# Where the sums of w_down's quadrants are formed: in the steps of the down-projection or in those of the up-projection

## The chip, the cores and the metric

The kernel runs on one core of one Trainium2 chip. The core has a matrix engine (TensorE, PE in the profile; its weight loads are PEld), a vector engine (VectorE, DVE), a scalar engine (ScalarE, ACT), a general engine (GpSimd, POOL) and a sync engine (SyncE, SP) that here only issues DMA transfers; POOL issues some as well. The metric is the device time of one execution in microseconds, the median of a few runs.

## The reference, cut to what matters

One layer of a bidirectional encoder on 2048 tokens of width 1024: a normalised input projection, windowed attention beside a state-space branch, an output projection with residual, and then a gated feed-forward block with a convolution of width 3 over the tokens. The change lies in the feed-forward block:

```
    h = rms_norm(x, norm_ffn_g)                                # [2048, 1024]
    up = depthwise_conv(h @ w_up, conv_w, conv_b)              # [2048, 5632]
    gate, val = up[..., :2816], up[..., 2816:]
    x = x + (silu(gate) * val) @ w_down                        # w_down [2816, 1024]
    return rms_norm(x, norm_final_g)
```

All arrays are float32.

## The kernel before, in words

The first 800 us or so compute everything up to the feed-forward block. The block is one loop, `steps`, of 68 steps and a last half step. Steps 0 to 43 are the up-projection: 22 feature blocks of 128 gate and 128 value features for the first 1024 tokens, then the same 22 for the second 1024. Steps 44 to 67 are the down-projection, in three chunks of w_down's rows (`DN` = 3, 4, 4 and `DF` = 0, 6, 14: a chunk c has 2 x DN[c] blocks of 128 rows, starting at block DF[c]), each chunk in eight steps of two token blocks of 128. A chunk's result is added to that of the chunk before, which lies in DRAM (x1_d, then sum_d; `rest` loads it), and the last chunk ends in the final norm (`last_rows`).

Each step is a product of 2 x 2 quadrants done with seven products of quadrants in place of eight, in the manner of Strassen and Winograd. One side (the stationary operand, `stationary`) is formed anew in each step from what the step loads: the weights of w_up (`uraw`, two loads of 512 KB) or the activations (`araw`). The other side (the moving operand, seven tiles `self.bop`, names in `BOP`) stays for a whole run of steps: quadrants of the normalised tokens in the up-projection, quadrants of w_down and their sums in the down-projection. Four of the seven are sums: t1, t2, t3, t4. Each operand is split into a high and a low part (`...h` by ACT at L1026, `...l` by DVE at L1027), and every product of quadrants is made of three passes, high by high, high by low and low by high (L1091).

The seven products of a step are interleaved by hand with the two (numbers 4 and 3) left over from the step before; `cur` is the step, `old` the one before. Their results meet in two sets of three PSUM banks (px, py, pz) and are added up by DVE (L1111 to L1134); L1131 is the addition that frees py for product 4. In the up-projection `up_conv` then does the convolution and the gate for the step before, and POOL stores the activations to DRAM (L1202, one store for each of the 44 steps). In chunks 0 and 1 of the down stage POOL stores the partial sums (L1141).

At the last step of a run of steps, `put` re-loads each of the seven moving operands for the next run as soon as its last product is done: from DRAM into a raw buffer (`braw`, L995), split by ACT (L997) and DVE (L998). The raw buffers are three, of 512 KB, in the pool `fr`.

`down_sums(c)` forms the sums t1 to t4 of w_down's quadrants for chunk c, in DN[c] parts. A part takes all three buffers of `fr` (tag `braw`, names `bsum`): A and B are loaded with one row block of 128 from the upper and the lower half of the chunk (L1066, SP, 512 KB each); C is empty. Four DVE subtractions and additions of 128 x 512 follow (L1067 to L1070), and POOL stores the four sums to DRAM (L1072, 256 KB each), from where `put` loads them. `sums` chains the parts of the three chunks, eleven in all, and after each step whose number is in `SUMS` one `next(sums)` writes one part into the program: behind steps 26, 30 and 34 the three parts of chunk 0, behind 45 to 48 the four of chunk 1, behind 53 to 56 the four of chunk 2.

The order of the instructions on an engine, and that of the DMA issues on SP and POOL, is fixed before the run by the tile framework, which may move an instruction ahead of others that are written before it where its inputs and buffers allow; on the chip each engine goes through its list in order and waits on semaphores. A tile gets its buffer when the last user of the buffer's tile before is done.

Of the kernel before, what the change touches and what calls it, by code (L numbers as in the profile page):

```python
# [39 lines left out]
TAB = [1] * 16  # L40
DN = [3, 4, 4]
DF = [0, 6, 14]
SUMS = [26, 30, 34, 45, 46, 47, 48, 53, 54, 55, 56]
HALF = 512
BLK = 1024
BOP = ["11", "t2", "21", "t1", "t3", "t4", "22"]
# [9 lines left out]
class Net:  # L56
# [1001 lines left out]
    def down_sums(self, c):  # L1058

        nc = self.nc  # L1060
        V = nc.vector
        n, f0 = DN[c], DF[c]
        for k in range(n):
            A, B, C = (self.fr.tile([128, 2, HALF], F32, tag="braw", name=self.nm("bsum")) for _ in range(3))
            for t, f in ((A, f0 + k), (B, f0 + n + k)):
                nc.sync.dma_start(t.rearrange("p n c -> p (n c)"), self.a["w_down"][128 * f:128 * (f + 1), :])  # L1066
            V.tensor_tensor(C[:, 0], A[:, 1], A[:, 0], op=ALU.subtract)  # L1067
            V.tensor_tensor(C[:, 1], B[:, 1], A[:, 1], op=ALU.subtract)
            V.tensor_tensor(A[:, 0], C[:, 1], A[:, 0], op=ALU.add)
            V.tensor_tensor(B[:, 0], B[:, 0], A[:, 0], op=ALU.subtract)  # L1070
            for m, t in (("t1", C[:, 0]), ("t3", C[:, 1]), ("t2", A[:, 0]), ("t4", B[:, 0])):
                nc.gpsimd.dma_start(self.wsum_d[c][m][:, k], t)  # L1072
            yield

    def steps(self, p, ps):
# [21 lines left out]
        for n, at in enumerate(todo + [None]):  # L1097
# [37 lines left out]
            if old:  # L1135
# [6 lines left out]
                else:  # L1142
                    self.last_rows(f_, old["gc"], p, 2)
            if n in SUMS:
                next(sums)
# [188 lines left out]
```

## Time and profile before

| what | value |
|---|---|
| median of 3 runs | 2186.12 us (2183.91 to 2192.61) |
| the profiled execution | 2188.02 us, span 2186.2 us |
| PE busy | 2074.0 us, 95% of the span |
| PE weight load busy | 1672.5 us, 77% |
| DVE busy | 1738.7 us, 80% |
| ACT busy | 1048.1 us, 48% |
| POOL busy | 140.4 us, 6% |
| mean granted TensorE clock | 0.982 of full speed |
| data moved | 337.97 MB, 155 GB/s |

The profiled execution is one run with the hardware profiler; its span is from the first to the last instruction, and its own time has a little around that. Busy shares are means over stages with different limits, so the views below go by stretches. A busy PE need not be a PE at full speed: the granted clock stands beside it. In rows of a timeline the bracket at the end is the idle time of that engine in front of the instruction, with what ended it.

### The profile page before, as it was taken

How to read it: one execution, taken by the hardware profiler on the slowest of the kernel's cores; microseconds unless marked ns; L12 is line 12 of the kernel's file. 1: busy time of each engine (PE TensorE's matmuls, PEld its weight loads, DVE VectorE, ACT ScalarE, POOL GpSimd, SP SyncE). 2: the span in 40 equal slices, each digit the busy share in tenths (PEclk: the TensorE clock that was granted, in tenths of full speed). 3: DMA queues.
4: the chain of work that ended last, by engine and by line, in shares of the span. 5: the costliest groups of instructions: out<-in, count | busy, mean ns of one | idle time of the engine just before them, and what ended most of it. 6: DMA issues, size and time to landing. Idle time of an engine off the chain costs nothing.

```text
span 2186.2 us, 27988 instructions
## 1 busy us (share of the span) xinstructions
PE 2074.0 (95%) x10000; PEld 1672.5 (77%) x10000; DVE 1738.7 (80%) x3065; ACT 1048.1 (48%) x1836; POOL 140.4 (6%) x230
## 2 busy tenths in 40 slices
PE   7998889799999997999999999999999999899997
PEld 5777777577777776888888878888888777777786
DVE  8978888675566557888888899888888978767875
ACT  5424444776666654544444464444445424224332
POOL 1300000000000000000000001000000010100111
PEclk9999999999999998999999999999999999999999
DMA  8965665523243238422222254322222798777542
GB/s 282 338 189 154 194 179 169 162 94 92 78 130 116 82 102 256 157 82 82 78 87 87 87 183 164 130 87 85 80 87 70 248 315 292 265 230 231 187 158 93
DMA packets 208939, 337.97 MB, mean 155 GB/s; under 512 B 13856, under 2 KB 135200, under 8 KB 208800
## 3 DMA queue, kind: packets, MB, share of 16 engines
q1 hardware_dynamic: 189072, 270.58, 39.4%
q0 software_dynamic: 16288, 62.92, 7.6%
q10 hardware_dynamic: 3440, 2.69, 0.4%
q8 instruction: 78, 1.28, 0.3%
q14 instruction: 61, 0.50, 0.1%
HBM read 231.81 MB, written 104.33 MB: 154 GB/s over the span
## 4 chain that ended last, share of the span: by engine, by line
issue 40%; PE 14%; POOL 2%; DMA 2%; DVE 1%; ACT 0%; POOLq 0%; ACTq 0%; SPq 0%; DVEq 0%
PE py L1091 6%; PE px L1091 4%; PE pz L1091 4%; POOL act L1202 1%; DMA braw<-ws2t 1%; POOL sum L1141 0%; POOL ws1t L1072 0%; DMA bsum<-in_w_down_dram 0%; DMA braw<-in_w_down_dram 0%; POOL ws0t L1072 0%; DMA ws2t<-bsum 0%; POOL ws2t L1072 0%; DVE bt L998 0%; DVE cu L1131 0%; ACT bt L997 0%
## 5 line engine op out<-in xcount | busy, mean ns | idle before, releaser
L1091 PE MATMUL px<-b,g1h 128*128 128x512 f32 x1056 | 328.6, 392 | 1.4 <-ACT cu L1109 1.4
L1091 PEld LDWEIGHTS px<-b,g1h 128*128 128x128 f32 x1056 | 199.9, 190 | 43.8 <-ACT cu L1109 2.3
L1091 PE MATMUL px<-b,g1l 128*128 128x512 f32 x528 | 207.6, 393 | 5.6 <-DVE g1l L1027 5.6
L1091 PE MATMUL py<-bt,g2h 128*128 128x512 f32 x528 | 168.4, 400 | 14.9 <-DVE cu L1131 14.9
L1091 PE MATMUL py<-bt,s2h 128*128 128x512 f32 x528 | 164.5, 393 | 4.0 <-ACT s2h L1026 4.0
L1091 PE MATMUL pz<-bt,s1h 128*128 128x512 f32 x528 | 163.2, 389 | 3.4 <-ACT s1h L1026 3.4
L1091 PE MATMUL pz<-b,s4h 128*128 128x512 f32 x528 | 162.9, 389 | 0.0
L1091 PE MATMUL py<-bt,s1h 128*128 128x512 f32 x528 | 162.7, 389 | 0.0
L1091 PEld LDWEIGHTS py<-bt,g2h 128*128 128x128 f32 x528 | 101.3, 193 | 39.5 <-DVE cu L1131 12.5
L1026 ACT ACTIVATE s1h<-st 128x1024 fp32r<-128x1024 f32 (+1 forms) x68 | 70.4, 1035 | 121.5 <-PE py L1091 108.1
L1091 PEld LDWEIGHTS px<-b,g1l 128*128 128x128 f32 x528 | 100.2, 190 | 28.5 <-DVE g1l L1027 7.5
L1091 PEld LDWEIGHTS py<-bt,s2h 128*128 128x128 f32 x528 | 98.9, 189 | 27.3 <-ACT s2h L1026 7.3
L1091 PEld LDWEIGHTS pz<-bt,s1h 128*128 128x128 f32 x528 | 99.0, 188 | 24.3 <-ACT s1h L1026 3.8
L1091 PEld LDWEIGHTS py<-bt,s1h 128*128 128x128 f32 x528 | 99.1, 188 | 20.6
L1091 PEld LDWEIGHTS pz<-b,s4h 128*128 128x128 f32 x528 | 99.1, 188 | 20.6
L78 PE MATMUL po<-wo,oh 128*128 128x512 f32 x256 | 112.2, 438 | 0.0
L1116 DVE TENSOR_TENSOR cu<-py,cu 128x512 f32<-128x512 f32 x68 | 46.9, 690 | 79.4 <-PE py L1091 79.3
L1091 PE MATMUL py<-bt,s2l 128*128 128x512 f32 x264 | 104.0, 394 | 2.4 <-DVE s2l L1027 2.2
L1091 PE MATMUL py<-bt,g2l 128*128 128x512 f32 x264 | 105.3, 399 | 0.0
L80 PE MATMUL po<-wo,ol 128*128 128x512 f32 x256 | 103.1, 403 | 0.0
L1091 PE MATMUL pz<-b,s4l 128*128 128x512 f32 x264 | 102.7, 389 | 0.0
L1091 PE MATMUL pz<-bt,s1l 128*128 128x512 f32 x264 | 102.7, 389 | 0.0
(272 smaller groups left out, 5070.4 us busy)
## 6 DMA issues: line engine op xcount, KB each, us to landing
uraw<-in_w_up_dram SPq DMA_DIRECT2D x88, 512.0 KB
araw<-act SPq DMA_DIRECT2D x32, 512.0 KB
xr<-sum SPq DMA_DIRECT2D x32, 512.0 KB
xr<-in_xT_dram SPq DMA_DIRECT2D x30, 512.0 KB
braw<-bop_d SPq DMA_DIRECT2D x28, 512.0 KB
act<-cv POOLq DMA_DIRECT2D x22, 512.5 KB, 2.9
bsum<-in_w_down_dram SPq DMA_DIRECT2D x22, 512.0 KB
act<-cv POOLq DMA_DIRECT2D x22, 511.5 KB, 3.3
```

The source lines that it names most:

```text
L78: nc.tensor.matmul(out, sh, mh, start=first and i == 0, stop=False)
L80: nc.tensor.matmul(out, sl, mh, start=False, stop=last and i == n - 1)
L1026: S.activation(h[:, :c], src, AF.Copy)
L1091: nc.tensor.matmul(bank, x[:, k], o[:, y, k], start=first and k == 0 and i == 0, stop=k == kn - 1 and i == 2, skip_group_check=True)
L1116: V.tensor_tensor(old["vc"][:, lo], old["Y"], old["vc"][:, lo], op=ALU.add)
L1202: nc.gpsimd.dma_start(self.act_d[c][f - DF[c], :, cols], va)
```

## The change

The list `SUMS` and one `yield`. Each part of `down_sums` is now written in two pieces: the two loads behind one step, the four DVE instructions and four stores behind the next. The eleven parts are written behind the pairs of steps 2 and 3, 5 and 6, 8 and 9, 11 and 12, 14 and 15, 17 and 18 (first 1024 tokens: the three parts of chunk 0 and three of chunk 1), and 24 and 25, 27 and 28, 30 and 31, 33 and 34, 36 and 37 (second 1024 tokens: the last of chunk 1 and the four of chunk 2). Nothing is computed that was not before, and nothing is left out.

```
-SUMS = [26, 30, 34, 45, 46, 47, 48, 53, 54, 55, 56]
+SUMS = [f + i for f in (2, 5, 8, 11, 14, 17, 24, 27, 30, 33, 36) for i in (0, 1)]
...
             A, B, C = (self.fr.tile([128, 2, HALF], F32, tag="braw", name=self.nm("bsum")) for _ in range(3))
             for t, f in ((A, f0 + k), (B, f0 + n + k)):
                 nc.sync.dma_start(t.rearrange("p n c -> p (n c)"), self.a["w_down"][128 * f:128 * (f + 1), :])
+            yield
             V.tensor_tensor(C[:, 0], A[:, 1], A[:, 0], op=ALU.subtract)
             V.tensor_tensor(C[:, 1], B[:, 1], A[:, 1], op=ALU.subtract)
             V.tensor_tensor(A[:, 0], C[:, 1], A[:, 0], op=ALU.add)
```

## Rows read from the trace of the kernel before

**Rows 1.** Stretches: busy us (count) of PE, PEld, DVE, ACT, POOL; clock, DMA share, GB/s.

```profile
1000.00:1280.00 280.00, 280.00 (x1237) 231.83 (x1236) 234.12 (x279) 130.33 (x181) 8.10 (x15) 1.00 0.26 91
1320.00:1380.00 60.00, 60.00 (x266) 49.47 (x265) 59.57 (x81) 30.05 (x40) 8.09 (x15) 1.00 0.50 171
1390.00:1690.00 300.00, 300.00 (x1325) 248.51 (x1324) 254.75 (x332) 145.06 (x189) 8.33 (x16) 1.00 0.24 82
1740.00:1800.00 60.00, 56.92 (x244) 45.07 (x244) 50.46 (x82) 14.09 (x23) 12.93 (x24) 1.00 0.92 320
1870.00:1930.00 60.00, 53.10 (x218) 42.78 (x217) 42.93 (x63) 13.36 (x18) 11.87 (x22) 0.94 0.79 257
1930.00:1990.00 60.00, 60.00 (x266) 49.67 (x266) 40.27 (x54) 14.50 (x19) 3.19 (x6) 1.00 0.65 204
```

**Rows 2.** Timeline of PE, 1740 to 1930 us, matmuls with idle time before them.

```profile
1778.22 0.74 PE L1091 MATMUL py<-bt,s2h 128*128 128x512 f32 x2 [0.86 <-ACT s2h L1026]
1792.83 0.50 PE L1091 MATMUL px<-b,g1l 128*128 128x512 f32 x1 [1.31 <-DVE g1l L1027]
1795.45 0.73 PE L1091 MATMUL py<-bt,s2h 128*128 128x512 f32 x2 [0.74 <-ACT s2h L1026]
1840.10 1.05 PE L1091 MATMUL py<-bt,g2h 128*128 128x512 f32 x2 [2.70 <-DVE cu L1131]
1846.96 0.73 PE L1091 MATMUL px<-b,g1h 128*128 128x512 f32 x2 [0.43 <-ACT cu L1109]
1864.60 1.19 PE L1091 MATMUL py<-bt,g2h 128*128 128x512 f32 x2 [4.11 <-DVE cu L1131]
1890.24 0.50 PE L1091 MATMUL py<-bt,s2l 128*128 128x512 f32 x1 [2.07 <-DVE s2l L1027]
1918.31 0.81 PE L1091 MATMUL py<-bt,g2h 128*128 128x512 f32 x2 [4.84 <-DVE cu L1131]
```

**Rows 3.** Timeline of DVE, first instruction of four of the parts.

```profile
1784.93 0.69 DVE L1067 TENSOR_TENSOR bsum<-bsum 128x512 f32<-128x512 f32 x1 [3.91 <-DMA bsum<-in_w_down_dram]
1888.29 0.69 DVE L1067 TENSOR_TENSOR bsum<-bsum 128x512 f32<-128x512 f32 x1 [5.11 <-DMA bsum<-in_w_down_dram]
1901.55 0.69 DVE L1067 TENSOR_TENSOR bsum<-bsum 128x512 f32<-128x512 f32 x1 [3.68 <-DMA ws2t<-bsum]
1916.96 0.69 DVE L1067 TENSOR_TENSOR bsum<-bsum 128x512 f32<-128x512 f32 x1 [6.48 <-DMA bsum<-in_w_down_dram]
```

**Rows 4.** Chain of waits, 1904 to 1934 us: start, duration, what.

```profile
1904.34 5.66 DMA ws2t<-bsum
...
1910.14 6.73 DMA bsum<-in_w_down_dram
...
1931.11 2.72 PE py L1091 x12
```

**Rows 5.** Short stretches behind gaps of PE; columns as in rows 1.

```profile
1890.00:1896.00 6.00, 5.76 (x18) 4.58 (x19) 6.00 (x10) 0.00 (x0) 1.32 (x3) 0.72 0.74 218
...
1840.00:1844.00 4.00, 3.90 (x10) 3.08 (x11) 3.19 (x5) 2.12 (x2) 0.00 (x0) 0.57 1.00 365
```

**Rows 6.** Stretches, tile bsum alone: busy us (count) of DVE, POOL; clock, DMA.

```profile
1320.00:1380.00 60.00, 8.18 (x12) 6.48 (x12) 1.00 0.50 171
1740.00:1930.00 190.00, 22.00 (x32) 17.29 (x32) 0.96 0.86 292
```

**Rows 7.** Timelines of DVE and PE in one step of the first half.

```profile
1111.50 0.68 DVE L1131 TENSOR_TENSOR cu<-py,cu 128x512 f32<-128x512 f32 x1
...
1116.31 0.62 PE L1091 MATMUL py<-bt,g2h 128*128 128x512 f32 x2
```

**Rows 8.** Timelines of POOL and DVE: activation stores, a part of chunk 0.

```profile
1369.49 0.54 POOL L1202 DMA_DIRECT2D act<-cv  x1 [10.60 <-DVE cv L1199]
1370.84 0.69 DVE L1067 TENSOR_TENSOR bsum<-bsum 128x512 f32<-128x512 f32 x1
...
1735.49 0.53 POOL L1202 DMA_DIRECT2D act<-cv  x1 [17.00 <-DVE cv L1199]
```

More of the change, by code (lines that the diff above doesn't have):

```diff
@@ L42 @@
 DF = [0, 6, 14]
-SUMS = [26, 30, 34, 45, 46, 47, 48, 53, 54, 55, 56]
+SUMS = [f + i for f in (2, 5, 8, 11, 14, 17, 24, 27, 30, 33, 36) for i in (0, 1)]
 HALF = 512
@@ L1066, in down_sums @@
                 nc.sync.dma_start(t.rearrange("p n c -> p (n c)"), self.a["w_down"][128 * f:128 * (f + 1), :])
+            yield
             V.tensor_tensor(C[:, 0], A[:, 1], A[:, 0], op=ALU.subtract)
```

## The prediction, made before the changed kernel was run

> **What bounds the kernel now.** I read the busy time by stretch first. In the up-projection TensorE (PE) is busy for every microsecond of the long stretches, 280.00 of 280.00 and 300.00 of 300.00, at the full granted clock [rows 1]. There only more work on PE's path, or a wait that reaches PE, can change the time. In the down stage two stretches differ: 56.92 of 60 us (1740 to 1800) and 53.10 of 60 us with a granted clock of 0.94 (1870 to 1930). The stretch behind them, with the same seven products a step and no sums, is full again: 60.00 of 60 [rows 1]. These two are the stretches in which the sums of chunks 1 and 2 run.
>
> Second, the timeline of PE, read only for idle time in front of a matmul. Between 1740 and 1930 us there are eight such gaps, all of them in [rows 2]. Three belong to the re-loading of the operands between chunk 0 and chunk 1 (2.70, 0.43 and 4.11 us). The other five, 0.86, 1.31, 0.74, 2.07 and 4.84 us, stand where the sums run.
>
> Third, the timeline of VectorE (DVE) at the sums [rows 3]. DVE works in order. At the first subtraction of a part (L1067) it stood still for 3.91, 5.11 and 6.48 us until the load of w_down had landed, and for 3.68 us until a store of the part before had landed. Behind that instruction stood s2l and g1l (the split stationaries) and the addition at L1131, and PE's gaps end on exactly these: 1792.83 on g1l, 1890.24 on s2l, 1918.31 on L1131 [rows 2]. So the chain is: store of part k lands, SP may issue the loads of part k+1 into the same three buffers, the load lands, DVE goes on, PE goes on. At 1916.96 the chain of waits shows it whole: 5.66 us of store, 6.73 us of load, then L1067 [rows 4].
>
> A stall is not a gap of its own length: 5.11 us cost PE 2.07 us and 6.48 us cost 4.84, while the 3.68 us at 1901.55 cost nothing. The steps of chunk 0, with three blocks in place of four, forgive less: 3.91 us cost 1.31 + 0.74.
>
> **What is removed.** Of the eleven parts, the eight of chunks 1 and 2 leave the down stage (chunk 0 was in the up-projection already). With them go the stalls, so these gaps: 0.86 + 1.31 + 0.74 + 2.07 + 4.84 = 9.82 us. Two of them were followed by a stretch at the lower clock: from 1890 to 1896 and from 1918 to 1924 the granted clock is 0.72 [rows 5], part of it at 1.2 in place of 2.4 GHz (one of the two windows stands there; the other reads the same 0.72). That is (1 - 0.72) x 6 = 1.68 us of lost matmul time each, 3.36 us together. Sum: 13.2 us. Lower bound: if the three short gaps in chunk 0, which are near to what an ordinary late split costs, stay, 10.3 us. SP also loses 16 loads there and POOL 32 store issues (17.29 us with their 22.00 us of DVE work [rows 6]). What is late next? Nothing that reaches PE: from 1930 to 1990, with the same loads of activations and partial sums at 204 GB/s and no parts, PE does not idle [rows 1].
>
> **What is added.** The same work, 22.00 us of DVE for eight parts, is 2.75 us a part [rows 6]; it goes beside PE in the up-projection, which DVE must have room for. DVE there is busy 234.12 of 280 us in the first half of the tokens and 254.75 of 300 in the second [rows 1]. A step is seven products of 2.72 us [rows 4], 19.04 us, so DVE's idle time in a step is 45.88 / 280 x 19.04 = 3.12 us in the first half and 45.25 / 300 x 19.04 = 2.87 us in the second. A part of 2.75 us fits either, the second with 0.12 us to spare, and some of that idle time is slivers that no instruction fits into. Beyond that DVE may be late: its addition L1131 starts at 1111.50 and takes 0.68 us, and the product that needs the bank it reads starts at 1116.31 [rows 7], 4.1 us later. Zero is the low end of the cost.
>
> Will they come in successive steps? The place in the text is not the place on the chip. The three parts of chunk 0 are written behind steps 26, 30 and 34. The third of them ran at 1370.84 us, right behind the store of the activations at 1369.49; nineteen more such stores follow, the last of the 44 (step 43's) at 1735.49, so that store is step 24's [rows 8]. A part written for step 34 ran ten steps early, and all three ran within 60 us [rows 6]. The order is fixed before the run, and the parts moved up to where buffers were free. So I expect six parts one after another behind the operand loads of the first half, and five behind those of the second. That is the densest case the rows know: from 1320 to 1380 DVE was busy 59.57 of 60 us with three parts, and PE 60.00 of 60 at clock 1.00 [rows 1]. This row decides for me: three successive parts on top of DVE's backlog from the operand loads cost nothing. The up-projection also has the bandwidth: 91 and 82 GB/s against 320 and 257 in the two stretches of the sums [rows 1]; a part adds two loads of 512 KB and four stores of 256 KB, 2 MB a step or some 110 GB/s.
>
> The queues. SP's loads of a part stand among the loads of w_up, which go into four buffers, two to a step, and so run a step ahead of their use; the part's loads wait for the stores of the part before. At the worst row (5.66 us for a store [rows 4]) w_up comes that much later out of a step of 19 us: nothing. On POOL the four store issues (17.29 / 32 = 0.54 us each [rows 6]) stand ahead of an activation store that nobody needs before the down stage. The extra yield puts a part's four DVE instructions a step behind its loads in the text. If the order keeps this, no part can wait for its load; if the parts move up as before, the distance is again what the order takes a load to cost, and here the bounds lie apart. In the up-projection the three parts had 0.00 us of such waits (DVE 59.57 of 60); in the down stage up to 6.48. I take zero. In the down stage DVE had so many holes (40.27 busy of 60 [rows 1]) that parts came 13.3 and 15.4 us apart in chunk 2 [rows 3], close to the 5.66 + 6.73 us of store and load. In the up-projection one hole of 3 us a step spaces them by about 19 us, which is beyond that.
>
> **The rivals.** (a) Some parts stall DVE in the up-projection as in the down stage: the first half of the tokens has no backlog behind which a load could land. Two stalls like that at 1888 cost 2 x (2.07 + 1.68) = 7.5 us: 2180.5. For it: DVE idles there in every step. Against it: loads there meet a third of the traffic.
> (b) Slower: the same stall at its worst, 6.48 us, part after part: 4.84 + 1.68 = 6.5 us each. From two of these on the gain is gone; with four of the eleven it is 26 us, and the time 2199. It needs stores and loads to take 12.4 us in the up-projection too, against which stand 82 to 91 GB/s.
> (c) More gain: the operand loads between chunk 0 and chunk 1 meet a DMA share of 1.00 at 1840 to 1844 [rows 5], with the gaps 2.70 + 0.43 + 4.11 [rows 2]. The granted clock of 0.57 there costs (1 - 0.57) x 4 = 1.7 us behind either long gap (the window at 1864 reads the same): 10.7 us in all. If less traffic and free buffers take half of that away, the time is 2168; all, 2162. Against it: the parts of chunk 1 are done by then, and those of chunk 2 come later.
> (d) The edit moves nothing that matters: the order lets the parts of chunks 1 and 2 drift to where they were. 2186. Against it: in the trace parts moved forward, never back.
> (e) POOL's store issues hold DVE, or the other way round. An issue of 0.54 us, four to a part, would make a part 2.75 + 4 x 0.54 = 4.91 us against idle times of 3.12 and 2.87: six parts make DVE 10.7 us late and five 10.2, less 4.1 us of room each: 12.7 us, so 2186. Against it: from 1320 to 1380 twelve such issues ran beside twelve such instructions, and PE lost nothing [rows 1, 6]. The Trainium skill (SBUF — State Buffer, Who interferes with whom) states that a DVE instruction with two SBUF inputs, as all four of a part are, and a GpSimd instruction that reads SBUF take an exclusive port in turn, the later one blocked for the whole of the other. By that rule such blocking would speak against putting more sums where DVE is fullest; that trace stretch does not show it for store issues.
>
> **How the numbers follow.** The profiled execution took 2188.02 us (span 2186.2), 1.9 us over the median of the three runs, 2186.12, and inside their spread of 2183.91 to 2192.61. On its own time the sum gives 2188.0 - 13.2 = 2174.8; on the median 2186.1 - 13.2 = 2172.9. I forecast 2173, with 2168 to 2178 as the range of this case (the lower bound 10.3 gives 2175.8, the rest is the spread of runs and small shifts in the order). Chances: forecast 0.57, (a) 0.19, (b) 0.06, (c) 0.12, (d) 0.04, (e) 0.02. The range of 8 in 10 is 2163 to 2187: it reaches from nearly the whole of (c) to (d). A measurement of this kernel tells 0.5%, 10.9 us, from no change; that line is at 2175.2 and cuts the forecast's own range. I give it two thirds on the fast side (0.38), (c) whole and a little of (a): 0.52 faster, 0.41 within, 0.07 slower.
>
> **What would show it.** In the changed kernel: no L1067 after 1690 us; PE without idle time in the steps that follow the operand loads of chunks 1 and 2; granted clock 1.00 there; the parts in two dense groups, behind the operand loads of either half, with DVE near full in them and PE busy throughout. I am wrong if PE idles in front of g1l, s2l or L1131's bank in the up-projection, if L1067 waits there for a load by more than 4 us, or if the gaps of the down stage stay without the parts.

## The result, and the profile after

The changed kernel takes 2176.2 us (median of 7 runs, 2173.63 to 2178.58) against 2186.12 us (median of 7, 2181.12 to 2192.61): 0.9948 of the time before, with a 95% interval of 0.9931 to 0.9965. That is 9.9 us less, with 13.2 forecast, inside the forecast's range of 2168 to 2178, 3 us above its middle, and right at the line of 0.5%. The profiled execution took 2178.58 us, 9.44 less than that of before. Behind this sum stand two terms, a larger gain than forecast and a loss that was forecast as zero.

In the new line numbers everything from the first subtraction on is one higher (L1067 is now L1068, L1091 is L1092, L1131 is L1132). Stretches of the changed kernel, columns as in [rows 1]:

```profile
900.00:1030.00 130.00, 124.71 (x535) 100.41 (x534) 114.15 (x145) 53.53 (x77) 16.27 (x30) 0.99 0.52 177
1320.00:1420.00 100.00, 100.00 (x442) 82.56 (x441) 98.33 (x135) 47.21 (x63) 13.64 (x26) 1.00 0.52 181
...
1740.00:1800.00 60.00, 58.90 (x247) 48.05 (x248) 48.46 (x76) 16.70 (x26) 4.80 (x9) 0.94 0.68 217
1870.00:1930.00 60.00, 60.00 (x263) 49.44 (x263) 42.83 (x58) 15.81 (x21) 3.20 (x6) 0.99 0.55 173
```

The two stretches of the down stage that had holes [rows 1] have none now that the sums would explain: the second is full, and what is left of the first, 1.10 us in front of a matmul at 1743.28 and the clock of 0.94, comes 3 us behind a gap of 3.25 us at 1739.91, where the re-loading in front of chunk 0 ends. The kernel before has the same gap at 1734.11, just ahead of its stretch. The new hole is in the first line: from 900 to 1030 us, where the six parts of the first half run, TensorE idles 5.29 of 130 us. The second line is the group of parts in the second half; DVE is nearly full there, and TensorE does not idle.

Which instructions wait? Timeline of DVE in the changed kernel, first subtraction of parts 3 to 6 and of two parts in the second half, with the instructions between parts 3 and 4:

```profile
932.79 0.69 DVE L1068 TENSOR_TENSOR bsum<-bsum 128x512 f32<-128x512 f32 x1 [3.00 <-DMA ws0t<-bsum]
...
946.99 0.68 DVE L1070 TENSOR_TENSOR bsum<-bsum,bsum 128x512 f32<-128x512 f32 x1
947.71 0.69 DVE L1071 TENSOR_TENSOR bsum<-bsum,bsum 128x512 f32<-128x512 f32 x1
948.32 0.68 DVE L1117 TENSOR_TENSOR cu<-py,cu 128x512 f32<-128x512 f32 x1
948.92 0.68 DVE L1027 TENSOR_TENSOR g2l<-uraw,g2h 128x512 fp32r<-128x512 f32 x1
950.32 1.28 DVE L1187 SCALAR_TENSOR_TENSOR cv<-cu,cw,cv 128x1023 f32<-128x1023 f32 x1 [0.72 <-ACT cv L1185]
954.40 0.69 DVE L1068 TENSOR_TENSOR bsum<-bsum 128x512 f32<-128x512 f32 x1 [2.80 <-DMA ws0t<-bsum]
...
976.25 0.69 DVE L1068 TENSOR_TENSOR bsum<-bsum 128x512 f32<-128x512 f32 x1 [3.03 <-DMA ws1t<-bsum]
...
997.93 0.69 DVE L1068 TENSOR_TENSOR bsum<-bsum 128x512 f32<-128x512 f32 x1 [2.87 <-DMA ws1t<-bsum]
...
1387.91 0.69 DVE L1068 TENSOR_TENSOR bsum<-bsum 128x512 f32<-128x512 f32 x1 [0.35 <-DMA ws2t<-bsum]
...
1407.03 0.69 DVE L1068 TENSOR_TENSOR bsum<-bsum 128x512 f32<-128x512 f32 x1 [0.63 <-DMA ws2t<-bsum]
```

Four parts wait 2.80 to 3.03 us, and not for a load: for a store of the part before. The timelines of POOL and of SP's queue beside them show which:

```profile
947.97 0.54 POOL L1073 DMA_DIRECT2D ws0t<-bsum  x1 [1.86 <-DVE bsum L1070]
948.70 0.54 POOL L1073 DMA_DIRECT2D ws0t<-bsum  x1 [0.18 <-issue]
...
947.70 0.33 SPq L1066 DMA_DIRECT2D bsum<-in_w_down_dram  x1
...
953.19 0.33 SPq L1066 DMA_DIRECT2D bsum<-in_w_down_dram  x1
```

The three buffers of a part come free one after the other: that of C when L1070 ends (947.67), and A of the next part is loaded into it at 947.70; that of A when the store issued at 947.97 has landed, and the next B is loaded there at 953.19; that of B last, when the store issued at 948.70 has landed. This last one becomes the next C, which nothing loads, but which the first subtraction writes. DVE reaches L1068 at 951.60 and stands until 954.40, 5.7 us behind the issue of the store.

With that, as an estimate from these rows, a step of 19.04 us grows by 2.75 us of part and 3.0 us of wait, less 3.12 us of idle time: 2.63 us. That gives 21.67 us; the parts above are 21.61, 21.85 and 21.68 us apart. From the first of these waits on DVE has no room left to be late, and TensorE waits. Timeline of PE in the changed kernel, the matmuls with idle time before them:

```profile
940.67 0.50 PE L1092 MATMUL py<-bt,s2l 128*128 128x512 f32 x1 [0.90 <-DVE s2l L1027]
957.48 0.50 PE L1092 MATMUL px<-b,g1l 128*128 128x512 f32 x1 [0.21 <-DVE g1l L1027]
960.63 0.73 PE L1092 MATMUL py<-bt,s2h 128*128 128x512 f32 x2 [0.59 <-ACT s2h L1026]
962.29 0.50 PE L1092 MATMUL py<-bt,s2l 128*128 128x512 f32 x1 [0.92 <-DVE s2l L1027]
984.13 0.50 PE L1092 MATMUL py<-bt,s2l 128*128 128x512 f32 x1 [0.91 <-DVE s2l L1027]
1001.01 0.50 PE L1092 MATMUL px<-b,g1l 128*128 128x512 f32 x1 [0.25 <-DVE g1l L1027]
1004.17 0.73 PE L1092 MATMUL py<-bt,s2h 128*128 128x512 f32 x2 [0.60 <-ACT s2h L1026]
1005.81 0.50 PE L1092 MATMUL py<-bt,s2l 128*128 128x512 f32 x1 [0.92 <-DVE s2l L1027]
```

These are 5.30 us in all. Six of the eight end on s2l and g1l, the split stationaries that stand behind the parts on DVE (4.11 us), two on s2h, which ACT splits from a sum that DVE forms (1.19 us).

To weigh loss and gain against each other I use three spans of each profiled execution. A runs from the first of the 44 activation stores on POOL to the ninth (the first group of parts), B from the ninth to the last (the rest of the up-projection), C from the last to the end of the span (the down stage). The time up to the first store is left out: between single profiles it varies from 901 to 911 us, in work that no kernel here changes, but for part 1: in the changed kernel its first instruction runs at 896.77 us, ahead of that store. The kernels of the experiments stand in the same table; each ratio is to the kernel before on the same chip.

| kernel | A | B | C | profiled execution | median | ratio, 95% |
|---|---|---|---|---|---|---|
| before | 150.20 | 677.25 | 450.71 | 2188.02 | 2186.12 | |
| after | 158.36 | 676.91 | 435.51 | 2178.58 | 2176.20 | 0.9948, 0.9931 to 0.9965 |
| e1_dense | 149.62 | 676.62 | 436.95 | 2167.15 | 2170.83 | 0.9929, 0.9916 to 0.9942 |
| e2_paced | 150.11 | 676.25 | 432.27 | 2170.30 | 2168.51 | 0.9919, 0.9904 to 0.9933 |
| e3_noyield | 157.41 | 677.79 | 438.04 | 2177.85 | 2177.42 | 0.9955, 0.9938 to 0.9973 |
| e4_inplace | 149.07 | 677.99 | 435.09 | 2172.35 | 2167.84 | 0.9920, 0.9906 to 0.9934 |
| e5_down_paced | 149.83 | 677.66 | 433.73 | 2174.42 | 2168.38 | 0.9918, 0.9904 to 0.9933 |
| e6_second | 149.95 | 677.32 | 453.84 | 2194.16 | 2191.02 | 1.0014, 1.0002 to 1.0026 |
| e7_more_work | 153.74 | 677.36 | 434.99 | 2169.60 | 2175.91 | 0.9951, 0.9933 to 0.9968 |
| e8_empty_first | 157.01 | 676.13 | 434.22 | 2174.96 | 2173.70 | 0.9942, 0.9926 to 0.9958 |
| e9_paced_inplace | 149.62 | 676.66 | 438.94 | 2167.99 | 2165.17 | 0.9903, 0.9886 to 0.9919 |

For the change that is 8.16 us lost in A, 0.34 gained in B and 15.20 gained in C. With the 2.0 us by which its first store came earlier they make the 9.4 us between the two profiled executions.

TensorE's own steps show more finely where the time went. The table has the start of the product of s4 in the same step of both profiled executions (matmul pz<-b,s4h on PE), and in one row the last activation store:

| place | before | after | the changed kernel is |
|---|---|---|---|
| ahead of the four waits | 912.30 | 909.21 | 3.09 us earlier |
| behind the last gap of the first group | 1007.50 | 1013.65 | 6.15 us later |
| last activation store | 1735.49 | 1741.29 | 5.80 us later |
| early in chunk 0 | 1754.10 | 1761.98 | 7.88 us later |
| chunk 0, behind the sums that ran there before | 1830.66 | 1833.38 | 2.72 us later |
| chunk 1, ahead of the stalls | 1876.68 | 1878.85 | 2.17 us later |
| chunk 1, behind them | 1925.50 | 1916.93 | 8.57 us earlier |
| chunk 2, behind the re-loading | 2064.66 | 2055.19 | 9.47 us earlier |

In the first half TensorE lost 9.24 us, 1.1 more than A shows: the first store, at which A begins, came only 2.02 us earlier where TensorE was 3.09 us ahead, as part 1 ran in front of it on DVE. The gaps alone do not make this up, because a gap costs more than its length: the step with the one gap of 0.90 us lasts 20.24 us (928.25 to 948.49), 1.20 more than 19.04. Behind that gap the next matmul of the pass comes 0.80 us later (940.67 to 941.47), where the others come 0.68 apart.

### The profile page after: what moved, and what is told of

Same layout as the page of the kernel before. It is cut to its first block, busy times and chain, and to the rows that moved or that the text cites. A ratio compares the mean times of both kernels' runs of the same rounds, so it can differ in the third digit from the quotient of the medians.

```text
span 2176.8 us, 27985 instructions
## 1 busy us (share of the span) xinstructions
PE 2077.6 (95%) x10000; PEld 1675.0 (77%) x10000; DVE 1741.6 (80%) x3065; ACT 1047.9 (48%) x1836; POOL 142.0 (7%) x230
## 4 chain that ended last, share of the span: by engine, by line
PE 46%; DVE 5%; issue 4%; DMA 3%; ACT 1%; POOL 1%; POOLq 0%; ACTq 0%; DVEq 0%
PE py L1092 20%; PE px L1092 13%; PE pz L1092 13%; DMA braw<-bop_d 1%; DMA braw<-in_w_down_dram 1%; DMA braw<-ws2t 1%; DVE b L998 1%; DVE bt L998 0%; ACT bt L997 0%; DVE cv L1187 0%; DVE cu L1132 0%; DMA braw<-ws1t 0%; DVE s1l L1027 0%; DMA ws1t<-bsum 0%; DVE g1l L1027 0%
## 5 line engine op out<-in xcount | busy, mean ns | idle before, releaser
L1092 PE MATMUL px<-b,g1h 128*128 128x512 f32 x1056 | 329.7, 393 | 2.5 <-ACT cu L1110 2.5
L1092 PEld LDWEIGHTS px<-b,g1h 128*128 128x128 f32 x1056 | 200.6, 190 | 45.3 <-ACT cu L1110 3.4
L1092 PE MATMUL px<-b,g1l 128*128 128x512 f32 x528 | 207.9, 394 | 3.7 <-DVE g1l L1027 3.7
L1092 PE MATMUL py<-bt,g2h 128*128 128x512 f32 x528 | 164.1, 391 | 9.1 <-DVE cu L1132 9.0
L1092 PE MATMUL py<-bt,s2h 128*128 128x512 f32 x528 | 166.6, 397 | 2.9 <-ACT s2h L1026 2.9
L1092 PE MATMUL pz<-bt,s1h 128*128 128x512 f32 x528 | 163.5, 390 | 3.2 <-ACT s1h L1026 3.2
L1092 PE MATMUL pz<-b,s4h 128*128 128x512 f32 x528 | 163.0, 389 | 1.0 <-DVE cu L1133 1.0
L1092 PE MATMUL py<-bt,s1h 128*128 128x512 f32 x528 | 162.7, 389 | 0.0
L1092 PEld LDWEIGHTS py<-bt,g2h 128*128 128x128 f32 x528 | 98.8, 188 | 32.3 <-DVE cu L1132 6.5
L1092 PEld LDWEIGHTS py<-bt,s2h 128*128 128x128 f32 x528 | 100.4, 191 | 26.4 <-ACT s2h L1026 5.5
L1092 PEld LDWEIGHTS px<-b,g1l 128*128 128x128 f32 x528 | 100.3, 190 | 26.3 <-DVE g1l L1027 5.3
L1092 PEld LDWEIGHTS pz<-bt,s1h 128*128 128x128 f32 x528 | 99.1, 188 | 24.5 <-ACT s1h L1026 4.0
L1092 PEld LDWEIGHTS pz<-b,s4h 128*128 128x128 f32 x528 | 99.0, 188 | 22.0 <-DVE cu L1133 1.5
L1092 PEld LDWEIGHTS py<-bt,s1h 128*128 128x128 f32 x528 | 99.1, 188 | 20.6
L1092 PE MATMUL py<-bt,s2l 128*128 128x512 f32 x264 | 105.3, 399 | 3.6 <-DVE s2l L1027 3.6
L1092 PE MATMUL py<-bt,g2l 128*128 128x512 f32 x264 | 103.1, 390 | 0.0
L1092 PE MATMUL pz<-b,s4l 128*128 128x512 f32 x264 | 102.7, 389 | 0.0
L1092 PE MATMUL pz<-bt,s1l 128*128 128x512 f32 x264 | 102.7, 389 | 0.0
L1092 PE MATMUL py<-bt,s1l 128*128 128x512 f32 x264 | 102.7, 389 | 0.0
```

The source lines that it names most:

```text
L1092: nc.tensor.matmul(bank, x[:, k], o[:, y, k], start=first and k == 0 and i == 0, stop=k == kn - 1 and i == 2, skip_group_check=True)
```

## The experiments

Theory: where the sums stand matters only through DVE's waits. The order, fixed beforehand, puts the first subtraction of a part where the store of the part before has not landed, and DVE, in order, holds the splits back. Rivals: the DVE work of the parts is itself too much for a dense group of steps; the store and load traffic slows the up-projection; the `yield`, in the wrong place, causes the wait; and for the gain: the down stage has no room for the sums at all, so that only moving them helps.

**One part in each step, placed behind an addition (e1_dense).** `issue_after` keeps what is written under it behind the instruction `mark` in the order. In each of the steps 3 to 8 and 25 to 29 the DVE instructions of one part are written, with the loads of the next behind them: groups as dense as those of the change, but at a fixed place in the step.

```
-SUMS = [f + i for f in (2, 5, 8, 11, 14, 17, 24, 27, 30, 33, 36) for i in (0, 1)]
+SUMS = [f + i for f in (2, 3, 4, 5, 6, 7, 24, 25, 26, 27, 28) for i in (0, 1)]
...
-                V.tensor_tensor(vc[:, hi], Z, vc[:, lo], op=ALU.add)
+                mark = V.tensor_tensor(vc[:, hi], Z, vc[:, lo], op=ALU.add).ins
...
-            if n in SUMS:
-                next(sums)
+            for _ in range(SUMS.count(n)):
+                with self.tc.issue_after(mark):
+                    next(sums)
```

> One part in each of the successive steps 3 to 8 and 25 to 29, each part's four DVE instructions queued behind the step's last addition (L1133 of the changed kernel), so that 19 us lie between two parts. Theory S (the loss in the first half is the wait of a part's first subtraction for the last store of the part before, 3.0 us in a step in which DVE has 3.12 us of idle time for 2.75 us of work): no such wait, no gap of PE between 900 and 1030 us, and the 8.9 us that the up-projection lost come back: 2167 us (2164 to 2170). Rival F (DVE has no room for 2.75 us of work in successive steps, the wait only stands where the room ends): the gaps stay in the same number of steps, 2174 to 2180 us.

Stretch of this kernel over the first group, as the first line of the changed kernel's stretches:

```profile
900.00:1030.00 130.00, 130.00 (x575) 107.69 (x574) 121.60 (x153) 60.43 (x85) 14.63 (x27) 1.00 0.45 162
```

TensorE is busy for all of it, while DVE does more here than in the change (121.60 against 114.15 us) and the traffic is close (162 against 177 GB/s). A is 149.62, the loss is gone, and C keeps its gain. Dense work and dense traffic are not what costs; the wait is. The median, 2170.83, lies 0.8 us above the range expected.

**The written steps, held (e2_paced).** The pairs of steps of the change, with the same `mark`, so that the parts cannot move up.

```
             if n in SUMS:
-                next(sums)
+                with self.tc.issue_after(mark):
+                    next(sums)
```

> The parts as the changed kernel writes them, in every third step, but held there: the four DVE instructions of a part are queued behind the last addition of their step. Theory S: no waits for stores, no gaps in the up-projection, 2167 us (2164 to 2170). Rival F: a third of the load on DVE in a step, so the gaps go as well: 2167. If the time stays at 2176, neither holds, and the work itself costs wherever it stands.

A is 150.11, with 130.00 of 130 us of TensorE and 118 GB/s. The time, 2168.51, is level with e1_dense within the intervals: once no part waits, spreading them out brings nothing that can be measured.

**Without the yield (e3_noyield).** Loads, instructions and stores of a part are written together behind the second step of each pair.

```
-SUMS = [f + i for f in (2, 5, 8, 11, 14, 17, 24, 27, 30, 33, 36) for i in (0, 1)]
+SUMS = [3, 6, 9, 12, 15, 18, 25, 28, 31, 34, 37]
...
-            yield
```

> The changed kernel without the added yield: loads and sums of a part are written behind the same step (3, 6, 9, 12, 15, 18, 25, 28, 31, 34, 37). Theory S: what sets the order is the buffers, not the place in the text, so the same 3 us waits for a store in the first half and the same time, 2176 us (2173 to 2179). Rival Y (the yield keeps the sums behind their loads): the first subtractions wait for loads by 2 to 6 us in the first half, and the time rises to 2180 or more.

Timeline of DVE, first subtraction of parts 4 and 5 (this kernel has the old line numbers):

```profile
950.98 0.69 DVE L1067 TENSOR_TENSOR bsum<-bsum 128x512 f32<-128x512 f32 x1 [2.83 <-DMA ws0t<-bsum]
...
972.89 0.69 DVE L1067 TENSOR_TENSOR bsum<-bsum 128x512 f32<-128x512 f32 x1 [3.09 <-DMA ws1t<-bsum]
```

The same waits for the same stores, and A is 157.41. The `yield` neither causes the wait nor prevents it: both pieces moved up together, and a distance between load and use cannot help against a wait for a store.

**Sums in place, two buffers (e4_inplace).** No empty buffer, so the first subtraction writes where its own load has just landed; the order is left free as in the change.

```
-            A, B, C = (self.fr.tile([128, 2, HALF], F32, tag="braw", name=self.nm("bsum")) for _ in range(3))
+            A, B = (self.fr.tile([128, 2, HALF], F32, tag="braw", name=self.nm("bsum")) for _ in range(2))
...
-            V.tensor_tensor(C[:, 0], A[:, 1], A[:, 0], op=ALU.subtract)
-            V.tensor_tensor(C[:, 1], B[:, 1], A[:, 1], op=ALU.subtract)
-            V.tensor_tensor(A[:, 0], C[:, 1], A[:, 0], op=ALU.add)
+            V.tensor_tensor(B[:, 1], B[:, 1], A[:, 1], op=ALU.subtract)
+            V.tensor_tensor(A[:, 1], A[:, 1], A[:, 0], op=ALU.subtract)
+            V.tensor_tensor(A[:, 0], B[:, 1], A[:, 0], op=ALU.add)
...
-            for m, t in (("t1", C[:, 0]), ("t3", C[:, 1]), ("t2", A[:, 0]), ("t4", B[:, 0])):
+            for m, t in (("t1", A[:, 1]), ("t3", B[:, 1]), ("t2", A[:, 0]), ("t4", B[:, 0])):
```

> A part forms its sums in place, in two buffers in place of three (t3 over B's lower half, t1 over A's, then t2 and t4 as before), with the same four DVE instructions. The empty third buffer, for which the first subtraction waited, is gone. Theory S: the next part's first load goes into the free third buffer at once, and only its second load waits for a store; if the order leaves a step between, no wait is left and the time is 2167 us (2164 to 2170); if it puts the first subtraction as close as now, that waits for store and load, 5 us or more, and the time is 2180 or more. Rival F: the DVE work is the same, 2174 to 2180.

Timeline of DVE, the longest wait of the first group; and the stretch over it:

```profile
995.78 0.69 DVE L1068 TENSOR_TENSOR bsum<-bsum,bsum 128x512 f32<-128x512 f32 x1 [1.37 <-DMA bsum<-in_w_down_dram]
```
```profile
900.00:1030.00 130.00, 130.00 (x575) 107.60 (x574) 121.79 (x153) 59.83 (x84) 16.86 (x31) 1.00 0.52 182
```

The wait for the store is gone; what is left are waits of up to 1.37 us for a load in this group, which DVE's idle time holds. The parts come as densely and with as much traffic (182 GB/s) as in the change, and TensorE loses nothing. This fits the reading that the wait was that for the empty buffer. The edit also leaves one of the three buffers free for the next load, and the run does not separate the two.

**The sums back in the down stage, held behind the mark (e5_down_paced).** The loop that writes the parts is that of e1_dense.

```
-SUMS = [f + i for f in (2, 5, 8, 11, 14, 17, 24, 27, 30, 33, 36) for i in (0, 1)]
+SUMS = [f + i for f in (25, 29, 33, 44, 45, 46, 47, 52, 53, 54, 55) for i in (0, 1)]
```

> The sums back in the down stage (chunk 1 in steps 44 to 48, chunk 2 in 52 to 56, chunk 0 in the up-projection near its old steps), but each part's four DVE instructions queued behind the last addition of the step after its loads, one part a step. The work and the DMA traffic of the kernel before, without its order. Theory S (the gaps of the down stage are stalls of DVE at a part's first subtraction): a step is 19 us in chunk 1 and 14.3 in chunk 0, a store and a load 12.4 us, so chunk 2's parts wait no longer and their 10.3 us come back, chunk 0's stretch at least in part: 2172 to 2176 us. Rival D (the gaps come from the traffic, 257 to 320 GB/s, or from the DVE work in those steps): the gaps stay, 2183 to 2188.

Stretches of this kernel where those of before had their holes [rows 1], and the first subtractions of three parts in the second of them:

```profile
1740.00:1800.00 60.00, 59.99 (x263) 49.10 (x263) 54.31 (x88) 16.67 (x27) 11.89 (x22) 0.99 0.94 324
1870.00:1930.00 60.00, 60.00 (x267) 49.65 (x266) 48.82 (x69) 14.37 (x20) 9.72 (x18) 1.00 0.73 248
```
```profile
1884.82 0.68 DVE L1068 TENSOR_TENSOR bsum<-bsum 128x512 f32<-128x512 f32 x1
...
1903.86 0.68 DVE L1068 TENSOR_TENSOR bsum<-bsum 128x512 f32<-128x512 f32 x1
...
1922.90 0.68 DVE L1068 TENSOR_TENSOR bsum<-bsum 128x512 f32<-128x512 f32 x1
```

The sums run where they ran before, beside the same 324 and 248 GB/s (320 and 257 in [rows 1]), and no part waits. C is 433.73, as good as with the sums moved away, and the time, 2168.38, is below the range expected. So the down stage did have room. What the change gained there is that it took the waits away, not the work; the move itself was not needed.

**All eleven parts in the second half (e6_second).** The change's free order, with other steps.

```
-SUMS = [f + i for f in (2, 5, 8, 11, 14, 17, 24, 27, 30, 33, 36) for i in (0, 1)]
+SUMS = [f + i for f in (22, 24, 26, 28, 30, 32, 34, 36, 38, 40, 42) for i in (0, 1)]
```

> The changed kernel with all eleven parts written in the second half's steps 22 to 43 (every second step). Theory S: the first three run in DVE's backlog from the operand loads and wait for nothing, the next two wait 0.4 to 0.6 us as now, and once the backlog is gone each of the other six waits some 3 us for the store of the part before: 2.75 + 3.0 us in a step with 2.87 us of idle time, 2.9 us a step, 17 us less the 4 us by which DVE may be late. First half without loss (-8.9 us), second half +13: 2176 + 4 = 2180 us (2176 to 2184). Rival H (only the first half has such waits, because of its start): no gaps in the second half, 2167 us.

A miss: 2191.02 us, a little slower than before. B is 677.32, so from the ninth store on the up-projection takes ten parts at no cost (of seven between 1380 and 1505 us two wait for nothing, four 0.42 to 0.72 us and one 1.02). The six waits of 3 us that were expected there did not come: in the second half the order leaves more work between the parts, and DVE reaches the first subtraction 5.2 and 5.5 us behind the issue of the last store (1477.94 to 1483.10, 1496.78 to 1502.26), where the change's first half has 2.9. The loss is in C, 453.84. DVE and PE, in the re-loading in front of chunk 0, and the stretch around it:

```profile
1750.78 0.69 DVE L1068 TENSOR_TENSOR bsum<-bsum 128x512 f32<-128x512 f32 x1
```
```profile
1750.08 1.52 PE L1092 MATMUL py<-bt,s1h 128*128 128x512 f32 x2 [4.14 <-ACT bt L997]
...
1756.61 0.80 PE L1092 MATMUL pz<-bt,s1l 128*128 128x512 f32 x1 [2.00 <-DVE s1l L1027]
```
```profile
1725.00:1775.00 50.00, 35.47 (x113) 23.29 (x113) 34.53 (x48) 16.97 (x24) 3.77 (x7) 0.83 0.67 223
```

The eleventh part ran among the loads of the operands, and a part takes all three raw buffers, through which `put` has to bring the operands in; TensorE idled 14.53 of 50 us at a clock of 0.83. SP issued no operand load between 1745.88 and 1755.08 us, and the part's stores went out from 1751.77 to 1754.85. So the trace reads as the buffers of the change's wait, missed here by another user; no run tests this apart.

**Twice the DVE work (e7_more_work).** As e1_dense, with the first two subtractions of each part done three times over.

```
+            for _ in range(3):
                 V.tensor_tensor(C[:, 0], A[:, 1], A[:, 0], op=ALU.subtract)
                 V.tensor_tensor(C[:, 1], B[:, 1], A[:, 1], op=ALU.subtract)
```

> The kernel with one part a step in successive steps (e1_dense), with the first two subtractions of each part done three times over, so that a part is eight DVE instructions, 5.5 us, in place of four; the result is the same. No part waits for a store. If DVE's idle time sets what a step can take, work beyond it costs as the wait did: six steps of 5.5 - 3.12 us and five of 5.5 - 2.87, 14.3 and 13.2 us, each less about 4 us of room: 2171 + 19 = 2190 us (2185 to 2194). If only waits on a store reach PE and work does not, 2171.

A miss on the small side: 2175.91 us, 5.1 more than e1_dense, which is not quite clear of noise (the two intervals meet); of the single profiled executions, A is 4.1 longer and B 0.7. A part is eight instructions, 8 x 0.69 = 5.5 us, against 3.12 us of idle time in a step, and yet the gaps of PE at the parts are small:

```profile
1021.42 0.50 PE L1093 MATMUL py<-bt,s2l 128*128 128x512 f32 x1 [0.41 <-DVE s2l L1027]
1041.62 0.50 PE L1093 MATMUL py<-bt,s2l 128*128 128x512 f32 x1 [0.41 <-DVE s2l L1027]
```

So 2.75 us more of work in each of eleven parts cost some 4.8 us in A and B, while 2.9 us of waiting in four parts cost the change 8.2. My reading, which no run shows, is that the order can lay work that it knows of between the instructions that matter, and cannot do so with a wait.

**C allocated first (e8_empty_first).** To see whether the empty buffer's turn can be changed by the place of its allocation.

```
-            A, B, C = (self.fr.tile([128, 2, HALF], F32, tag="braw", name=self.nm("bsum")) for _ in range(3))
+            C, A, B = (self.fr.tile([128, 2, HALF], F32, tag="braw", name=self.nm("bsum")) for _ in range(3))
```

> The changed kernel, with the empty buffer of a part created ahead of the two loaded ones, so that it gets the buffer that comes free first and the two loads get the ones that come free later; PE's order is the same, instruction by instruction. Theory S, sharpened: what PE loses is the wait that the order did not foresee. The first subtraction now needs a load that can only start when a store has landed, so it waits longer than 3.0 us wherever the order puts it as near as now, the gaps of the first half grow, and the time is 2178 to 2188 us. If the order moves the sums away from the loads far enough, the waits and gaps shrink, and the time is 2168 to 2174. Rival F (the DVE work alone sets the loss): 2176 as now, with the same gaps.

Timeline of DVE, part 4:

```profile
954.24 0.69 DVE L1068 TENSOR_TENSOR bsum<-bsum 128x512 f32<-128x512 f32 x1 [2.61 <-DMA ws0t<-bsum]
```

The waits stay (2.53, 2.61, 2.41 and 2.12 us in parts 3 to 6), A is 157.01, and the median is not to be told from that of the change. The loads of A and B go out as in the change, the first as C's old buffer comes free. So the place of the allocation in the text does not decide which buffer C gets; the time lies in the lower of the bands expected, but not for its reason, and the experiment decides nothing.

**Held and in place (e9_paced_inplace).** e2_paced and e4_inplace together.

> Both cures together: sums in place in two buffers, and each part's DVE instructions held behind the last addition of their step, every third step. Neither kernel alone had a wait of DVE that reached PE in the up-projection, so there is nothing left for the second to take away: 2168 us (2165 to 2171), as with either. If it is below 2164, the operand loads gain from the buffers too.

2165.17 us, 0.9903 of the time before (0.9886 to 0.9919), the lowest of all; A is 149.62. Its interval meets those of e1_dense, e2_paced, e4_inplace and e5_down_paced, so that it is the best of them is not shown, only that it beats the change.

More raw buffers, the other way to take the wait away, were not tried.

## Why the prediction was right in time, and wrong in one term

**What is removed** was right in place and mechanism: no L1068 after 1690 us, the five gaps gone, the clock in the second stretch 0.99 in place of 0.94. It was 15.20 us against 13.2. The table of TensorE's steps places the 2.0 us between them. Chunk 1 gained 10.74 us, where the sum had 2.07 + 4.84 + 3.36 = 10.27. Chunk 0 gained 5.16, where it had 2.91 for the gaps alone; but the entry into it lost 2.08, at the lower clock shown above (0.94). The two re-loadings behind it gained 0.55 and 0.90 us, which the sum had at nothing: the gaps of the first went from 2.70 + 0.43 + 4.11 [rows 2] to 2.04 + 0.57 + 3.87, rival (c) at less than a tenth of what it offered. C of the kernels without waits in it spreads from 432.27 to 438.94, so differences of this size may be chance. That the sums had to leave the down stage was never claimed, but the argument read as if the stage were too full for them, and e5_down_paced shows that it was not.

**What is added** failed, at "I take zero" for the waits of the parts, and one of the prediction's own signs of being wrong came true: PE idled in front of s2l and g1l in the up-projection. The sentence before it set the spacing of parts, about 19 us, against 5.66 + 6.73 us of store and load. The spacing was right, but it is that of the starts. The four DVE instructions of a part are spread over 15.6 us of the step (932.79 to 948.40), and from the last of them to the next first subtraction there are 3.2 us, less than the 5.66 us of a store alone [rows 4]. [Rows 3] already had such a wait on a store, 3.68 us at 1901.55, and I had passed over it as one that cost nothing. The dense stretch of before [rows 1], which "decides for me", had only three parts, behind a backlog of DVE; it held for the second half, where the parts wait 0.63 us at most and B loses nothing, and not for the first. What sets the halves apart is where the order puts the next first subtraction: in the second half DVE reaches it 5.4 us behind the issue of the last store (1401.02, below, to 1406.40), in the first 2.9 us (948.70 to 951.60), and the store issued at 948.70 took 5.7 us.

```profile
1401.02 0.54 POOL L1073 DMA_DIRECT2D ws2t<-bsum  x1 [1.26 <-DVE bsum L1071]
```

**Rival (a)** came true in its effect, with a store in place of a load: four waits of about 2.9 us in place of two of 5.11, 8.16 us in place of 7.5. My time for it, 2180.5, was 4.3 us high; on the profiled executions it would be 2182.3 against 2178.58, and there the larger gain in C and the earlier first store make the difference. **Rival (b)**, four stalls at 6.5 us each, overpriced them about three times: 8.16 / 4 = 2.0 us each by A, 2.3 by TensorE's steps. Its bound, stores and loads in series, does not hold at these four waits, since only the store is waited for. **Rival (d)** fell: the parts ran in two dense groups, as expected. **Rival (e)** fell: L1071, with both inputs from SBUF, takes 0.69 us at 947.71 while POOL's store issue runs from 947.97 to 948.51, as long as everywhere else. The Trainium skill (SBUF — State Buffer, Who interferes with whom) also infers that what GpSimd needs to issue a DMA is the write side of the shared port, which such an instruction doesn't take; the row agrees with that.

So the forecast is near by luck, because two errors have opposite signs. On the profiled executions, where the sum gave 2174.8 and 2178.58 was measured, the 3.8 us between them are 8.16 of loss, less 2.0 of additional gain in C, 0.34 in B and the 2.02 of the earlier first store.

Of the 9.24 us that TensorE lost in the first half, 5.30 are gaps and some 1.8 clock (below); the other 2.1 I put down to what a gap costs beyond its length, 0.30 us at the one shown above.

## What to carry to other kernels

For a group of buffers that is used again and again, find the user that comes free last and the first instruction of the next round that touches it, be it a write into a buffer that nobody loads, and set the distance between these two, not between the starts of two rounds, against the time of the store. When an in-order engine stalls at such a place, holding the instruction to a later place in the step, or doing the work in place so that the buffer isn't needed, gives back as much as moving the whole work to another stage. Before moving work out of a stage that has holes in it, ask whether the work or its wait makes the holes: a part that waits for nothing ran beside a full TensorE in either stage.

## What the runs showed of the hardware that was not expected

Short stretches of the changed kernel, columns as in [rows 1]:

```profile
940.00:960.00 20.00, 19.12 (x82) 15.24 (x82) 16.45 (x23) 6.74 (x11) 2.17 (x4) 1.00 0.54 177
960.00:980.00 20.00, 18.49 (x74) 14.79 (x74) 16.22 (x21) 7.10 (x11) 2.71 (x5) 0.91 0.56 184
962.00:966.00 4.00, 3.71 (x10) 2.94 (x11) 4.00 (x6) 1.63 (x3) 0.00 (x0) 0.62 0.38 132
1004.00:1024.00 20.00, 18.92 (x82) 15.38 (x83) 19.12 (x23) 9.47 (x14) 1.82 (x4) 1.00 0.58 197
```

A gap of 0.90 us at 940.67 left the granted clock at full speed (1.00 from 940 to 960). Two gaps of 0.59 and 0.92 us, less than 2 us apart, were followed by 0.62 from 962 to 966, a part of it at 1.2 in place of 2.4 GHz; over 960 to 980 that is (1 - 0.91) x 20 = 1.8 us, more than the two gaps. In the prediction I had counted such a price only for gaps of 2 us and above. But two gaps of the same size and as close, 0.60 and 0.92 us at 1004.17 and 1005.81, left the clock at 1.00 (1004 to 1024), and so did the six such pairs in the first group of e3_noyield and e8_empty_first. So short gaps can be followed by the lower clock, once in eight such pairs here; what decides it, the runs do not settle.
